# RMS normalisation: other cuts of the first and third tile's loads, and of the first groups

## The chip, the cores and the metric

The kernel runs on one core of a Trainium2 chip. The metric is the device time of one execution in microseconds (us). Three runs of the kernel before gave a median of 161.39 us (161.28 to 161.51). The profile covers one execution of its own; its span of 159.6 us is a little shorter than the time measured for that execution (161.33 us), as it begins and ends with the recorded work.

## The reference

The input x is 16 x 1024 x 512 in float32, gamma has 512 elements. Every row of 512 is divided by its root mean square, and multiplied by gamma:

```python
def reference(x, gamma):
    eps = 1e-5
    rms = np.sqrt(np.mean(x ** 2, axis=-1, keepdims=True) + eps)
    return (x / rms * gamma).astype(np.float32)
```

x is 33.55 MB, and so is the output, so 67.1 MB have to move.

## The kernel before

The 16,384 rows are cut into four tiles (t = 0 to 3), each of 128 partitions with R = 32 rows of 512. In what follows "a row" is one row in each of the 128 partitions, 128 x 512 x 4 bytes = 0.262 MB. Three slots in on-chip memory hold a tile each; tile 3 takes the slot of tile 0 again. Results are written in place, and stored from the slot.

All transfers are issued by SyncE, in the order of the program: one that waits holds back those behind it.

```python
xv = xf.rearrange("(t p r) d -> t p r d", p=P, r=R)
slots = [const.tile([P, R, D], fp32, name=f"slot{i}") for i in range(3)]

def load(t, slot, r0, r1):
    dma = nc.sync.dma_start(out=slots[slot][:, r0:r1], in_=xv[t][:, r0:r1])
    ...
gamma_row = const.tile([1, D], fp32)
pieces = (0, 128, 224, 320, 416, D)

load(0, 0, 0, 8)
for c0, c1 in zip(pieces, pieces[1:]):
    nc.sync.dma_start(out=gamma_row[:, c0:c1], in_=gamma.unsqueeze(0)[:, c0:c1])
load(0, 0, 8, 16)
load(0, 0, 16, 32)
load(1, 1, 0, 16)
load(1, 1, 16, 32)
```

Gamma, one row, is spread to all partitions by a matmul with a column of ones (`gamma_psum`), and copied once to on-chip memory (`gamma_b`) for GpSimd.

The work goes in groups (tile, first row, rows, pieces of the squares, rows for GpSimd):

```python
groups = [
    (0, 0, 7, (7,), 3),
    (0, 7, 9, (9,), 5),
    (0, 16, 16, (7, 9), 7),
    (1, 0, 16, (7, 9), 7),
    (1, 16, 16, (7, 5, 4), 7),
    ...            # (2, 0), (2, 16), (3, 0), (3, 16): 16 rows each, (7, 5, 4)
]
```

ScalarE squares a piece and DVE sums each row of it. The squares need a place: PSUM holds at most 7 rows, a tile of its own 5, and a piece of 9 is parked in the last rows of slot 2, which tile 2 is not yet in.

```python
def square_sums(ss, t, g, r, m, k):
    if m == 9:
        sq = slots[2][:, 23:32, :]
    else:
        home, name, most = ((psum, "sq_psum", 7), (const, "sq_sbuf", 5))[k % 2]
        sq = home.tile([P, most, D], fp32, name=name)
    rows = slots[slot_of[t]][:, g + r : g + r + m, :]
    nc.scalar.activation(out=sq[:, :m], in_=rows, func=AF.Square)
    nc.vector.tensor_reduce(out=ss[:, r : r + m, 0], in_=sq[:, :m], axis=mybir.AxisListType.X, op=OP.add)
```

The group's inverse root is taken by ScalarE (square root) and DVE (reciprocal). GpSimd multiplies the last `share` rows of the group by it and by gamma; for the others ScalarE does the first product, row by row, and DVE the second, with `gamma_psum`, in one instruction. Each engine runs in the order of the program, and the squares of the next group stand ahead of the scaling of this one:

```python
for k, group in enumerate(groups):
    ...
    scale_by_pool(rstd, t, g, n, share)       # GpSimd
    for piece in todo[:2]:
        square_sums(*piece)                   # next group: ScalarE, DVE
    scale(rstd, t, g, 0, half)                # ScalarE
    for piece in todo[2:]:
        square_sums(*piece)
    scale(rstd, t, g, half, mine)             # ScalarE
    times_gamma(t, g, 0, mine)                # DVE
    transfers(t, g)                           # SyncE
    for nxt in ahead:
        rstd = inverse_rms(ss, nxt[2])        # ScalarE, DVE
```

The stores and the later loads:

```python
def transfers(t, g):
    if (t, g) == (0, 0):
        store(0, 0, 0, 1)
        load(2, 2, 0, 16)
        store(0, 0, 1, 2)
        load(2, 2, 16, 23)
    elif (t, g) == (0, 16):
        store(0, 0, 2, 3)
        load(2, 2, 23, 32)
        store(0, 0, 3, 16)
        store(0, 0, 16, 32)
        load(3, 0, 0, 16)
        load(3, 0, 16, 32)
    elif (t, g) == (1, 16):
        store(1, 1, 0, 32)
    elif (t, g) == (2, 16):
        store(2, 2, 0, 32)
    elif (t, g) == (3, 0):
        store(3, 0, 0, 16)
    elif (t, g) == (3, 16):
        store(3, 0, 16, 32)
```

Here the load of tile 2's rows 23 to 32 has to wait until DVE has summed the last piece of 9 squares (group (1, 0)) out of these rows, and the first load of tile 3 until the store of the same rows of tile 0 has landed.

Of the kernel before, what the change touches and what calls it, by code (L numbers as in the profile page):

```python
# [9 lines left out]
def kernel(  # L10
# [6 lines left out]
    nc = tc.nc  # L17
# [8 lines left out]
    N, D = xf.shape  # L26
# [13 lines left out]
    slots = [const.tile([P, R, D], fp32, name=f"slot{i}") for i in range(3)]  # L40
# [3 lines left out]
    def load(t, slot, r0, r1):  # L44
        dma = nc.sync.dma_start(out=slots[slot][:, r0:r1], in_=xv[t][:, r0:r1])
        before_scale.append((slot, r0, r1, dma))

    def store(t, slot, r0, r1):
        dma = nc.sync.dma_start(out=ov[t][:, r0:r1], in_=slots[slot][:, r0:r1])
        before_scale.append((slot, r0, r1, dma))  # L50

    gamma_row = const.tile([1, D], fp32)
    pieces = (0, 128, 224, 320, 416, D)

    load(0, 0, 0, 8)
    for c0, c1 in zip(pieces, pieces[1:]):
        nc.sync.dma_start(out=gamma_row[:, c0:c1], in_=gamma.unsqueeze(0)[:, c0:c1])
    load(0, 0, 8, 16)
    load(0, 0, 16, 32)
    load(1, 1, 0, 16)  # L60
    load(1, 1, 16, 32)

# [11 lines left out]


    groups = [
        (0, 0, 7, (7,), 3),
        (0, 7, 9, (9,), 5),
        (0, 16, 16, (7, 9), 7),
        (1, 0, 16, (7, 9), 7),  # L80
        (1, 16, 16, (7, 5, 4), 7),
        (2, 0, 16, (7, 5, 4), 7),
# [4 lines left out]
    slot_of = [0, 1, 2, 0]  # L87

    def square_sums(ss, t, g, r, m, k):
        if m == 9:  # L90
            sq = slots[2][:, 23:32, :]
        else:
            home, name, most = ((psum, "sq_psum", 7), (const, "sq_sbuf", 5))[k % 2]
            sq = home.tile([P, most, D], fp32, name=name)
        rows = slots[slot_of[t]][:, g + r : g + r + m, :]
        nc.scalar.activation(out=sq[:, :m], in_=rows, func=AF.Square)  # L96
        nc.vector.tensor_reduce(  # L97
            out=ss[:, r : r + m, 0], in_=sq[:, :m], axis=mybir.AxisListType.X, op=OP.add
        )
# [29 lines left out]
    def transfers(t, g):  # L129
        if (t, g) == (0, 0):  # L130
            store(0, 0, 0, 1)
            load(2, 2, 0, 16)
            store(0, 0, 1, 2)
            load(2, 2, 16, 23)
        elif (t, g) == (0, 16):
            store(0, 0, 2, 3)
            load(2, 2, 23, 32)
            store(0, 0, 3, 16)
            store(0, 0, 16, 32)
            load(3, 0, 0, 16)  # L140
            load(3, 0, 16, 32)
        elif (t, g) == (1, 16):
# [7 lines that stand above are left out]
# [12 lines left out]
    for piece in todo:  # L162
        square_sums(*piece)
    rstd = inverse_rms(ss, groups[0][2])
    nc.scalar.copy(out=gamma_b[:, 0], in_=gamma_psum[:, 0])  # L165
    for k, group in enumerate(groups):
        t, g, n, pieces, share = group
        mine = n - share
        half = (mine + 1) // 2
        ahead = groups[k + 1 :][:1]  # L170
        ss, todo = pieces_of(ahead[0]) if ahead else (None, [])
        scale_by_pool(rstd, t, g, n, share)
        for piece in todo[:2]:
            square_sums(*piece)
        scale(rstd, t, g, 0, half)
        for piece in todo[2:]:
            square_sums(*piece)
        scale(rstd, t, g, half, mine)
        times_gamma(t, g, 0, mine)
        transfers(t, g)  # L180
        for nxt in ahead:
            rstd = inverse_rms(ss, nxt[2])
# [30 lines left out]
```

## Time and profile before

| what | value |
|---|---|
| time, median of 3 | 161.39 us |
| profile span | 159.6 us |
| DVE busy | 112.0 us, 70% |
| ScalarE (ACT) busy | 107.8 us, 68% |
| GpSimd (POOL) busy | 106.4 us, 67% |
| TensorE busy | 2.0 us, 1% |
| bytes read and written | 33.56 MB and 33.55 MB |
| mean over the span | 421 GB/s |
| 16 DMA engines' share, SyncE's queue | 98.2% |

An engine's line in the profile has its busy time, its share of the span and its instructions. In the timeline each line has start, duration, engine, line of the kernel, operation, output<-input and shapes; in square brackets stands the idle time before it and what ended it. SPq is SyncE's sequencer: its DMA lines show when a transfer was issued, not when its bytes moved. The DMA view lists issues with the KB of each and the time from issue to landing, that is, until its semaphore is complete. The slices cut the span into 40 equal parts of 4 us; the DMA digit is the busy share in tenths, and GB/s what was moved.

### The profile page before, as it was taken

The page shows a single profiled execution, that of the slowest core. Times are in us where ns is not written, and L with a number is a line of the kernel's source. Part 1 is how long each engine was busy: PE and PEld are TensorE (multiplying, and loading weights), DVE is VectorE, ACT ScalarE, POOL GpSimd, SP SyncE. Part 2 cuts the span into 40 slices and gives each one's busy share as a digit, 9 for nine tenths or more (in the row PEclk, how much of TensorE's full clock was granted, in tenths as well). Part 3 has the DMA queues.
Part 4 walks back from the last instruction along what each step waited for, and adds up shares of the span by engine and source line. Part 5 has one row for each costly group of instructions (what it writes and reads, how often), then busy time and mean ns, then how long its engine had stood idle before and what let it go on. Part 6 is the DMA issues. An engine that isn't in the chain of part 4 may idle for free.

```text
span 159.6 us, 275 instructions
## 1 busy us (share of the span) xinstructions
PE 2.0 (1%) x2; PEld 0.5 (0%) x2; DVE 112.0 (70%) x39; ACT 107.8 (68%) x108; POOL 106.4 (67%) x24
## 2 busy tenths in 40 slices
PE   0050000000000000000000000000000000000000
PEld 0010000000000000000000000000000000000000
DVE  0028097998898999999999999999999009700000
ACT  3072957967999998999899899989960990000000
POOL 1000942994999599999999999999999990000000
DMA  5999999999999999999999999996996997999995
GB/s 199 428 427 501 419 394 435 485 394 394 460 394 394 429 454 407 427 452 452 468 394 394 509 411 394 526 526 263 526 509 279 526 476 312 394 468 452 394 435 222
DMA packets 2747, 67.12 MB, mean 421 GB/s; under 512 B 313, under 2 KB 314, under 8 KB 698
## 3 DMA queue, kind: packets, MB, share of 16 engines
q1 hardware_dynamic: 2746, 67.11, 98.2%
q14 instruction: 1, 0.01, 0.0%
HBM read 33.56 MB, written 33.55 MB: 421 GB/s over the span
## 4 chain that ended last, share of the span: by engine, by line
DVE 59%; ACT 22%; DMA 4%; ACTq 0%; issue 0%
DVE ss L97 36%; DVE slot L122 23%; ACT slot L118 8%; ACT slot L96 7%; ACT sq_psum L96 6%; DMA slot<-in_x_dram 4%; DVE ss L103 1%; ACT ss L102 1%; ACTq L208 0%; ACT gamma_b L165 0%
## 5 line engine op out<-in xcount | busy, mean ns | idle before, releaser
L109 POOL TENSOR_TENSOR slot<-slot,ss 128x3584 f32<-128x3584 f32 (+2 forms) x9 | 46.9, 5214 | 23.7 <-DVE ss L103 23.7
L110 POOL TENSOR_TENSOR slot<-slot,gamma_b 128x3584 f32<-128x3584 f32 (+2 forms) x9 | 59.3, 6585 | 0.7
L97 DVE TENSOR_REDUCE ss<-sq_psum 128x7 f32<-128x3584 f32 (+1 forms) x13 | 42.2, 3246 | 13.2 <-ACT sq_psum L96 13.2
L118 ACT ACTIVATE slot<-slot,ss 128x512 f32<-128x512 f32 x75 | 47.2, 706 | 4.7 <-DVE ss L103 4.7
L122 DVE TENSOR_TENSOR slot<-slot,gamma_psum 128x4608 f32<-128x4608 f32 (+2 forms) x9 | 41.3, 4590 | 8.7 <-ACT slot L118 8.7
L96 ACT ACTIVATE sq_psum<-slot 128x3584 f32<-128x3584 f32 (+1 forms) x13 | 34.6, 2658 | 6.0 <-DMA slot<-in_x_dram 5.2
L97 DVE TENSOR_REDUCE ss<-slot 128x9 f32<-128x4608 f32 x3 | 14.9, 4953 | 4.4 <-ACT slot L96 4.2
L97 DVE TENSOR_REDUCE ss<-sq_sbuf 128x5 f32<-128x2560 f32 x5 | 14.0, 2802 | 0.0
L96 ACT ACTIVATE slot<-slot 128x4608 f32<-128x4608 f32 x3 | 12.1, 4032 | 0.0
L96 ACT ACTIVATE sq_sbuf<-slot 128x2560 f32<-128x2560 f32 x5 | 11.6, 2320 | 0.0
L102 ACT ACTIVATE ss<-ss,eps_t 128x16 f32<-128x16 f32 (+2 forms) x9 | 2.7, 304 | 11.9 <-DVE ss L97 11.9
L103 DVE RECIPROCAL ss<-ss 128x16 f32<-128x16 f32 (+2 forms) x9 | 2.1, 235 | 0.4 <-ACT ss L102 0.4
L66 PE MATMUL gamma_psum<-gamma_row,ones_col 1*128 1x512 f32 x2 | 2.0, 1121 | 8.7 <-DMA gamma_row<-in_gamma_dram 8.7
L72 ACT ACT_TABLE_LOAD x1 | 1.3, 1283 | 1.1 <-PEq L197 1.1
L165 ACT COPY gamma_b<-gamma_psum 128x512 f32<-128x512 f32 x1 | 0.6, 564 | 0.0
L66 PEld LDWEIGHTS gamma_psum<-gamma_row,ones_col 1*128 1x128 f32 x2 | 0.5, 304 | 8.7 <-issue 8.7
L64 POOL MEMSET ones_col<- 1x128 f32 x1 | 0.2, 194 | 0.3 <-POOLq L197 0.3
L197 POOL MEMSET const-float32-0.0<- 128x1 f32 x1 | 0.1, 98 | 0.2 <-issue 0.2
L72 ACT ACTIVATE table<-eps_t 128x1 f32<-128x1 f32 x1 | 0.2, 203 | 0.0
L197 POOL MEMSET const-bfloat16-1.0<- 128x1 bf16 x1 | 0.1, 101 | 0.0
L197 POOL MEMSET const-uint8-127<- 128x1 uint8 x1 | 0.1, 101 | 0.0
L197 POOL MEMSET const-float32-1.0<- 128x1 f32 x1 | 0.1, 98 | 0.0
(1 smaller groups left out, 0.1 us busy)
## 6 DMA issues: line engine op xcount, KB each, us to landing
slot<-in_x_dram SPq DMA_DIRECT2D x6, 4096.0 KB, 21.7
out_dram<-slot SPq DMA_DIRECT2D x3, 4096.0 KB, 21.9
slot<-in_x_dram SPq DMA_DIRECT2D x2, 2048.0 KB, 8.5
out_dram<-slot SPq DMA_DIRECT2D x1, 3328.0 KB, 21.7
slot<-in_x_dram SPq DMA_DIRECT2D x1, 2304.0 KB, 14.2
slot<-in_x_dram SPq DMA_DIRECT2D x1, 1792.0 KB
out_dram<-slot SPq DMA_DIRECT2D x3, 256.0 KB, 29.4
gamma_row<-in_gamma_dram SPq DMA_DIRECT2D x4, 0.4 KB
```

The costliest lines, as they stand in the source:

```text
L66: nc.tensor.matmul(gamma_psum[:, 0], ones_col, gamma_row, start=True, stop=True)
L72: nc.scalar.activation(out=table, in_=eps_t, func=AF.Sqrt)
L96: nc.scalar.activation(out=sq[:, :m], in_=rows, func=AF.Square)
L97: nc.vector.tensor_reduce(out=ss[:, r : r + m, 0], in_=sq[:, :m], axis=mybir.AxisListType.X, op=OP.add)
L102: nc.scalar.activation(out=ss[:, :n, 0], in_=ss[:, :n, 0], func=AF.Sqrt, bias=eps_t, scale=1.0 / D)
L103: nc.vector.reciprocal(out=ss[:, :n, 0], in_=ss[:, :n, 0])
L109: nc.gpsimd.tensor_tensor(out=part, in0=part, in1=by_row, op=OP.mult)
L110: last = nc.gpsimd.tensor_tensor(out=part, in0=part, in1=gamma_b.to_broadcast([P, share, D]), op=OP.mult)
L118: nc.scalar.activation(out=x[:, g + r, :], in_=x[:, g + r, :], func=AF.Copy, scale=rstd[:, r])
L122: scaled = nc.vector.tensor_tensor(out=part, in0=part, in1=gamma_psum.to_broadcast([P, r1 - r0, D]), op=OP.mult)
L165: nc.scalar.copy(out=gamma_b[:, 0], in_=gamma_psum[:, 0])
L197: nc = _bacc.Bacc("TRN2", target_bir_lowering=False, num_devices=1)
```

## The change

The change makes fewer and larger transfers in the beginning. Tile 0 comes in 12 and 20 rows in place of 8, 8 and 16. Its groups have 12, 10 and 10 rows in place of 7, 9 and 16, and two of them use pieces of 10 squares, which are parked in slot 2's last rows, 22 to 32, as the pieces of 9 are in 23 to 32. Gamma is one transfer in place of five. Of the three early single-row stores one is left. Tile 2 comes in 20 and 12 rows in place of 16, 7 and 9, the 20 after the first group and the 12 after the last group of tile 0. The stores of tile 0's other rows are cut at row 22 in place of row 16.

```diff
     gamma_row = const.tile([1, D], fp32)
-    pieces = (0, 128, 224, 320, 416, D)
-
-    load(0, 0, 0, 8)
-    for c0, c1 in zip(pieces, pieces[1:]):
-        nc.sync.dma_start(out=gamma_row[:, c0:c1], in_=gamma.unsqueeze(0)[:, c0:c1])
-    load(0, 0, 8, 16)
-    load(0, 0, 16, 32)
+
+    load(0, 0, 0, 12)
+    nc.sync.dma_start(out=gamma_row, in_=gamma.unsqueeze(0))
+    load(0, 0, 12, 32)
     load(1, 1, 0, 16)
     load(1, 1, 16, 32)
 ...
     groups = [
-        (0, 0, 7, (7,), 3),
-        (0, 7, 9, (9,), 5),
-        (0, 16, 16, (7, 9), 7),
+        (0, 0, 12, (7, 5), 5),
+        (0, 12, 10, (10,), 5),
+        (0, 22, 10, (10,), 5),
         (1, 0, 16, (7, 9), 7),
 ...
     def square_sums(ss, t, g, r, m, k):
-        if m == 9:
-            sq = slots[2][:, 23:32, :]
+        if m > 7:
+            sq = slots[2][:, 32 - m : 32, :]
 ...
         if (t, g) == (0, 0):
             store(0, 0, 0, 1)
-            load(2, 2, 0, 16)
-            store(0, 0, 1, 2)
-            load(2, 2, 16, 23)
-        elif (t, g) == (0, 16):
-            store(0, 0, 2, 3)
-            load(2, 2, 23, 32)
-            store(0, 0, 3, 16)
-            store(0, 0, 16, 32)
+            load(2, 2, 0, 20)
+        elif (t, g) == (0, 22):
+            load(2, 2, 20, 32)
+            store(0, 0, 1, 22)
+            store(0, 0, 22, 32)
             load(3, 0, 0, 16)
             load(3, 0, 16, 32)
```

## The prediction

> **What bounds the kernel now.** I read the page's slices and totals first, then the DMA issues one by one, then the timeline of the first 56 us. A row below means one row per partition: 128 x 512 floats, 0.262 MB, and the kernel moves 128 rows in and 128 rows out.
>
> ```profile
> DMA  5999999999999999999999999996996997999995
> GB/s 199 428 427 501 419 394 435 485 394 394 460 394 394 429 454 407 427 452 452 468 394 394 509 411 394 526 526 263 526 509 279 526 476 312 394 468 452 394 435 222
> ...
> HBM read 33.56 MB, written 33.55 MB: 421 GB/s over the span
> ```
>
> The DMA digits are 9 nearly everywhere. A single slice is not to be believed (526 beside 263 GB/s: whole packets are counted in one slice or the next), but the mean is. DVE, ScalarE and GpSimd are at 67 to 70%. The page's chain that ended last runs through DVE and ScalarE, because it follows semaphores back from the last store; it does not show that the store's bytes queued behind others. So I look at when each transfer lands. From the DMA views of short windows (size, then us from issue to landing), in order of issue:
>
> ```profile
> slot<-in_x_dram SPq DMA_DIRECT2D x1, 2048.0 KB, 7.1
> ...
> slot<-in_x_dram SPq DMA_DIRECT2D x1, 2048.0 KB, 9.8
> ...
> slot<-in_x_dram SPq DMA_DIRECT2D x1, 4096.0 KB, 19.2
> ...
> out_dram<-slot SPq DMA_DIRECT2D x1, 256.0 KB, 29.4
> ...
> slot<-in_x_dram SPq DMA_DIRECT2D x1, 2304.0 KB, 14.2
> ...
> out_dram<-slot SPq DMA_DIRECT2D x1, 4096.0 KB, 20.0
> ```
>
> Their issues stand in the timeline of SyncE at 0.74, 2.90, 3.29, 28.80, 49.40 and 138.76 us. Issue plus time to landing gives the landings, and summing the rows in program order gives how many rows had then gone through the queue: 8 rows at 7.84, 16 at 12.7, 32 at 22.5, 90 at 58.2, 99 at 63.6, and all 256 at 158.8. One straight line through first and last fits all: **landing of row n = 2.98 + 0.609 n us** (7.85, 12.7, 22.5, 57.8, 63.3, 158.9). A queue that had once run empty would have left a step. The kernel is bound by one queue that is never empty, at 0.262 MB / 0.609 us = 430 GB/s, and compute is hidden.
>
> The first load gives the cost of a cold start: 7.1 us for 8 rows, of which 8 x 0.609 = 4.87 is streaming and 2.23 is fixed. A transfer issued at t with n rows ahead of it therefore keeps to the line if t + 2.23 is no later than 2.98 + 0.609 n, that is, **issued by D(n) = 0.75 + 0.609 n**. The transfer to watch is the last piece of tile 2, which cannot be issued before DVE has summed the squares that were parked in its rows:
>
> ```profile
> 24.61 2.28 DVE L122 TENSOR_TENSOR slot<-slot,gamma_psum 128x2048 f32<-128x2048 f32 x1
> ...
> 24.94 3.14 ACT L96 ACTIVATE sq_psum<-slot 128x3584 f32<-128x3584 f32 x1
> ...
> 26.92 0.35 SPq L49 DMA_DIRECT2D out_dram<-slot  x1
> ...
> 40.36 4.03 ACT L96 ACTIVATE slot<-slot 128x4608 f32<-128x4608 f32 x1
> ...
> 44.42 4.95 DVE L97 TENSOR_REDUCE ss<-slot 128x9 f32<-128x4608 f32 x1
> ...
> 49.40 0.33 SPq L45 DMA_DIRECT2D slot<-in_x_dram  x1
> ```
>
> The reduce ends at 44.42 + 4.95 = 49.37 and the load is issued at 49.40. Ninety rows are ahead of it (64 of loads, then 1, 16, 1, 7 and 1), so D(90) = 55.6: 6.2 us to spare. That spare time is what hides the wait today.
>
> **What the Trainium skill says.** "DMA: Bandwidth & Descriptors", section Where 436 GB/s comes from, gives a ceiling of 435.2 GB/s for a core's DMA; the 430 GB/s of the line is within about 1% of it, so the only thing the change can win in the stream is about 67.1 MB / 435.2 = 154.2 against 256 x 0.609 = 155.9, 1.7 us. The same page, Anatomy of one DMA, says that any wait for a semaphore takes place on the issuing sequencer before dispatch; the trace agrees (the load is issued 0.03 us after the reduce), and it means that everything behind a waiting load in program order waits too. "SBUF — State Buffer", The DMA setup-cost knee, has about 2 us that don't scale with bytes; measured here, 2.23.
>
> **The change part by part.** Durations: ScalarE squares 3.14 us for 7 rows and 4.03 for 9, so 0.445 a row and 4.47 for 10; 2.32 for 5. DVE sums 3.83 to 3.89 for 7, 4.95 for 9, so 0.55 a row and 5.5 for 10; 2.80 for 5. DVE's product with gamma 2.28 for 4 rows, 4.94 for 9: 0.53 a row, 3.88 for 7, 2.81 for 5. ScalarE scales a row in 0.63.
>
> *Gamma in one piece* takes four issues of about 0.33 us off SyncE, 1.3 us in which the queue had 8 rows (4.9 us) to work on. The landings at 16 and 32 rows lie on the line, so the five pieces cost nothing visible. Worth: 0.
>
> *Loads in 12 and 20 rows.* The same bytes; but work waits for the whole of each. Twelve rows land at 2.98 + 7.31 = 10.3 (8 landed at 7.84, +2.4). The next 20 land together at row 32: 22.5, where rows 8 to 16 used to be there at 12.7. Step by step, in program order:
> - First group: squares of 7 rows 10.3 to 13.5, of 5 rows to 15.8; DVE sums 13.5 to 17.3 and to 20.1; root and reciprocal to 20.7 (15.5 before).
> - Second group: ScalarE would be free at 20.9 but its rows land at 22.5. Squares of 10 rows 22.5 to 27.0, sum 27.0 to 32.5, then the product with gamma of the first group's 7 rows 32.4 to 36.3 (it ended at 26.9 before).
> - The store of row 0 is issued at 36.3 and the 20-row load of tile 2 at 36.7, not at 26.9 and 27.3. With 64 rows ahead, D(64) = 39.7: 3.4 us to spare. No gap here.
> - Third group: ScalarE's root at 32.5, squares of 10 rows 32.7 to 37.2, sum 37.2 to 42.7, root, then tile 1's first 7 squares from 42.9 to 46.1 and its 9 squares, which are parked in tile 2's last rows, from 46.0 to 50.05. DVE sums the 7 until 50.0 and the 9 from 50.1 to **55.0** (49.37 before, +5.7).
>
> *Third tile in 20 and 12 rows, one early store.* The 12-row load waits for that sum and is issued at 55.06. Ahead of it lie 64 + 1 + 20 = 85 rows, 5 fewer than before, so D(85) = 52.5. **It is 2.55 us late**, and the queue is empty for that long: the 21-row and 10-row stores stand behind it on SyncE and can't fill the hole, although most of their rows are done.
>
> *Small stores.* Two fewer transfers of 2 KB per partition. The landings after the three early stores lie 0.3 to 0.4 us above the line (58.2 for 57.8; 63.6 for 63.3), so two of them may save 0.2.
>
> *After the hole.* The shift of compute: DVE's product for the third group is 5 rows, not 9, and ends at 58.2 instead of 54.9 (+3.3); ScalarE is 5.7 later when it begins tile 1's second half (55.7 for 50.0). Both engines are nearly full, so later groups run 3.3 to 5.7 us later. Does that open a second hole? The queue itself is 2.55 later. The first load of tile 3 goes when the 21-row store has landed: 118 rows, 2.98 + 71.9 + 2.55 = 77.4, against D(128) + 2.55 = 81.3. The store of tile 2 was issued at 111.19, so by 116.9, against D(192) + 2.55 = 120.2. The last store by 138.76 + 5.7 = 144.5 against D(240) + 2.55 = 149.5. All keep 3 us or more: no second hole, and none of the spare time gives the first one back.
>
> Sum: 161.39 + 2.55 - 0.2 = **163.7 us**, 1.4% slower.
>
> **Rivals.** (1) *The hole is hidden and the time stays at 161.4.* For it: the margin is a difference of two numbers near 54, and 2 us of error in either closes it; a somewhat slower stream in the first 50 us would do it (the landings run 0.4 late there). Against it: eight steps of the chain have measured durations, and only the 10-row forms are extrapolated, by one row. (2) *A second hole or a longer one*: if ScalarE's shift passes fully to the stores of tiles 2 and 3, or if the 36.7 us load misses its 3.4 us, each 1 us more adds 1 us: 165 or more. (3) *Faster*: fewer, larger transfers push the stream towards the ceiling. At most 1.7 us, if there were no hole at all: 159.7. The before's line leaves so little that over 2% (158.2 us) is out of reach. (4) *Compute becomes the bound*: it would need the last store's issue after 149.5; estimated at 144.5, so no.
>
> **Range and chances.** The chain of steps I trust to 0.7 us, the landing line to 0.4, a restart in mid-stream (both directions busy) to perhaps 0.5. That makes 162.2 to 165.0. Slower by over 2% begins at 164.6: one chance in seven. Faster by over 2%: one in a hundred.
>
> **What would show it.** In the changed kernel's trace: first squares at 10.3, second group's at 22.5 and waiting for a load; row 0's store at 36.3; the sum of the 9 squares ending at 55.0 and the 12-row load issued right after it; that load landing 9.5 us after issue (2.23 + 12 x 0.609), cold, instead of queued; landings on the old line before it and 2.4 us above it up to the last. The prediction is wrong if landings stay on one line (rival 1), or if a second step shows at tile 2's or tile 3's stores (rival 2).

## The result, and the profile after

The changed kernel takes **165.53 us** (165.51 to 165.58), 4.1 us more than before; the ratio is 1.0256 with an interval of 1.0239 to 1.0274. That is slower by over 2%, and above the predicted range of 162.2 to 165.0.

The page of the changed kernel, busy share and rate of the DMA engines in slices of 4.1 us:

```profile
DMA  5999999999999399999999999999989969899994
GB/s 194 468 429 480 440 416 392 440 456 384 384 480 480 96 408 264 504 431 410 400 440 440 400 456 424 448 448 512 416 352 512 480 288 512 384 400 464 416 432 208
```

The 14th slice (53.2 to 57.3 us) has a 3 and 96 GB/s where the digit was 9 before: here the queue ran empty. A slice counts a packet where it begins (a full share of 1.78 stands beside an empty slice further below), so its width is not to be taken from here.

The timeline of the changed kernel: start, duration, engine, operation.

```profile
10.59 3.16 ACT L93 ACTIVATE sq_psum<-slot 128x3584 f32<-128x3584 f32 x1 [7.95 <-DMA slot<-in_x_dram]
...
22.70 4.47 ACT L93 ACTIVATE slot<-slot 128x5120 f32<-128x5120 f32 x1 [1.50 <-DMA slot<-in_x_dram]
...
50.29 4.95 DVE L94 TENSOR_REDUCE ss<-slot 128x9 f32<-128x4608 f32 x1
...
36.52 0.35 SPq L49 DMA_DIRECT2D out_dram<-slot  x1
...
55.27 0.33 SPq L45 DMA_DIRECT2D slot<-in_x_dram  x1
```

All of compute's steps stand within 0.3 us of where they were predicted: 10.6 for 10.3, 22.7 for 22.5 with ScalarE idle for 1.50 us on the 20-row load, 36.5 for 36.3, and the sum of the nine squares ends at 55.24 for 55.0. The late load is issued at 55.27.

What differs is the landings. From the DMA view of the changed kernel, the 20-row load issued at 36.91, the late load (55.27), the 21-row store behind it (55.70), and the last store (143.38):

```profile
slot<-in_x_dram SPq DMA_DIRECT2D x1, 5120.0 KB, 18.0
...
slot<-in_x_dram SPq DMA_DIRECT2D x1, 3072.0 KB, 11.0
...
out_dram<-slot SPq DMA_DIRECT2D x1, 5376.0 KB, 23.4
...
out_dram<-slot SPq DMA_DIRECT2D x1, 4096.0 KB, 19.5
```

Row 85 lands at 54.9 (the old line says 54.7), row 97 at 66.3 (62.1), row 118 at 79.1 (74.8), row 256 at 162.9 (158.9). So **one step, between rows 85 and 97**: 11.4 us from landing to landing, where 12 rows take 7.3. It is 4.1 us, as much as the time that was lost; after it the landings run beside the old line, 4.0 to 4.6 us above it.

The first load of this kernel, issued at 0.74, also brings 12 rows and also starts with nothing ahead of it:

```profile
slot<-in_x_dram SPq DMA_DIRECT2D x1, 3072.0 KB, 9.8
```

So the late load, with 11.0 us, is 1.2 us slower than a cold start of its own size. The 9.5 us expected for it came from the first load of the kernel before, and that load's fixed part of 2.23 us is at the low end: in the sixteen traces of this case the first load's time less 0.609 us a row is 2.2 to 2.6 us, here 9.8 - 7.3 = 2.5.

### The profile page after: what moved, and what is told of

Read it like the earlier page. It is cut to its first block, busy times and chain, and to the rows that moved or that the text cites. A ratio compares the mean times of both kernels' runs of the same rounds, so it can differ in the third digit from the quotient of the medians.

```text
span 163.8 us, 260 instructions
## 1 busy us (share of the span) xinstructions
PE 2.0 (1%) x2; PEld 0.5 (0%) x2; DVE 112.2 (69%) x39; ACT 107.9 (66%) x108; POOL 106.4 (65%) x24
## 4 chain that ended last, share of the span: by engine, by line
DVE 51%; ACT 23%; DMA 13%; SPq 0%; ACTq 0%; issue 0%
DVE ss L94 31%; DVE slot L119 19%; DMA slot<-in_x_dram 13%; ACT slot L115 8%; ACT slot L93 8%; ACT sq_psum L93 5%; ACT sq_sbuf L93 1%; ACT ss L99 1%; DVE ss L100 1%; ACTq L202 0%; SPq L45 0%; SPq L55 0%
## 5 line engine op out<-in xcount | busy, mean ns | idle before, releaser
L94 DVE TENSOR_REDUCE ss<-sq_psum 128x7 f32<-128x3584 f32 (+1 forms) x12 | 38.4, 3200 | 15.3 <-ACT sq_psum L93 15.3
L119 DVE TENSOR_TENSOR slot<-slot,gamma_psum 128x4608 f32<-128x4608 f32 (+3 forms) x9 | 41.3, 4590 | 8.3 <-ACT slot L115 8.3
L93 ACT ACTIVATE sq_psum<-slot 128x3584 f32<-128x3584 f32 (+1 forms) x12 | 31.4, 2616 | 8.6 <-DMA slot<-in_x_dram 7.9
L94 DVE TENSOR_REDUCE ss<-slot 128x10 f32<-128x5120 f32 (+1 forms) x3 | 15.9, 5308 | 7.1 <-ACT slot L93 7.0
L94 DVE TENSOR_REDUCE ss<-sq_sbuf 128x5 f32<-128x2560 f32 x6 | 16.8, 2804 | 0.0
L93 ACT ACTIVATE slot<-slot 128x5120 f32<-128x5120 f32 (+1 forms) x3 | 12.9, 4317 | 1.5 <-DMA slot<-in_x_dram 1.5
L93 ACT ACTIVATE sq_sbuf<-slot 128x2560 f32<-128x2560 f32 x6 | 13.9, 2320 | 0.0
```

Of the source, the lines that this page charges most:

```text
L119: scaled = nc.vector.tensor_tensor(out=part, in0=part, in1=gamma_psum.to_broadcast([P, r1 - r0, D]), op=OP.mult)
```

## The experiments

To compare runs I use that step: the time from the landing of the transfer ahead to the landing of the late load, less 0.609 us a row. "Late by" is the issue time plus the cold start's fixed 2.23 us, less the landing of the transfer ahead; negative if the load came in time. With a fixed part of 2.5 us all these figures would be 0.3 us larger.

**Fill the empty stretch.** The 21-row store, ready long before, goes ahead of the late load:

```diff
-            load(2, 2, 20, 32)
             store(0, 0, 1, 22)
+            load(2, 2, 20, 32)
```

> Theory (the loss is one empty stretch of the queue behind the late 12-row load, with the slow restart that follows it): the 21-row store, ready at about 47 us, goes ahead of that load, so 106 rows are ahead of it and it may be issued up to 65.3 us; it is issued near 55.3, nothing runs empty, and all of the 4.1 us comes back: 161.4 us, within 0.4. Rival (about half of the loss lies in other parts of the change: one gamma transfer, fewer early stores, larger pieces): 163 us or more.

162.11 us, ratio 1.0034 (1.0017 to 1.0051). The store is issued at 46.77, the load still at 55.19, and the DMA view of this kernel shows it queued behind other work:

```profile
out_dram<-slot SPq DMA_DIRECT2D x1, 5376.0 KB, 21.6
...
slot<-in_x_dram SPq DMA_DIRECT2D x1, 3072.0 KB, 20.2
```

From the store's landing (68.37) to the load's (75.39) is 7.02 us for 12 rows: no step. 3.6 of the 4.1 us come back with nothing changed but the order of two transfers, and the rival, that half of the loss lies in the pieces, falls. Half a microsecond stays, a little more than the 0.4 that the theory allowed. It is not lost at the late load: this kernel's landings lie 0.4 us above the line at row 85, ahead of that load, and 1.1 us above it at row 144.

**More or fewer rows ahead of the late load.** Tile 2 in 22 and 10 rows, or 16 and 16:

```diff
-            load(2, 2, 0, 20)
+            load(2, 2, 0, 22)        # second kernel: 0, 16
 ...
-            load(2, 2, 20, 32)
+            load(2, 2, 22, 32)       # second kernel: 16, 32
```

> The early load of tile 2 takes 22 rows and the late one 10, nothing else changes. Theory (lateness plus a fixed slow restart of 1.4 us): two more rows ahead shorten the empty stretch by 2 x 0.609 = 1.2 us: 164.3 us. Rival (the slow restart grows with the length of the empty stretch): more than 1.2 us comes back, 163.8 us or less. Rival (the loss is elsewhere): no change, 165.5.

164.11 us, ratio 1.0137 (1.0051 to 1.0222). Late by 1.4, step 2.6.

> The early load of tile 2 takes 16 rows and the late one 16. Theory: four rows fewer ahead lengthen the empty stretch by 4 x 0.609 = 2.4 us: 168.0 us, with the slow restart still about 1.4 us of it. Rival (slow restart in proportion): 169.3 us. Rival (the loss is elsewhere): 165.5.

167.93 us, ratio 1.037 (1.0298 to 1.0442). Late by 5.0, step 6.5. Over these three kernels (20, 22 and 16 rows) the step is the lateness plus 1.2 to 1.5 us, whatever the lateness is: a fixed extra, which the prediction didn't have.

**An earlier late load.** Tile 0 in three loads, so that the second group needn't wait for row 32:

```diff
-    load(0, 0, 12, 32)
+    load(0, 0, 12, 22)
+    load(0, 0, 22, 32)
```

> Tile 0 comes in 12, 10 and 10 rows, so that the second group's rows land near 16.5 us and not 22.7. Theory: ScalarE begins the second group at 20.9, 1.8 us earlier, every step up to the late load moves with it, the load is issued at 53.5 and not 55.3, and 1.8 us comes back: 163.7 us. Rival (the second group isn't what sets the late load): 165.5 us.

164.94 us, ratio 1.0184 (1.0113 to 1.0255). The chain of steps moved as expected: the second group's squares begin at 21.01, the late load is issued at 53.58, 1.7 us earlier. But only 0.6 us came back (0.8 if each kernel is compared with the runs of the kernel before beside it). The load took 12.2 us from issue to landing, not 11.0: late by 0.8, step 3.4. The fixed extra was no longer fixed.

**What the extra belongs to.** In the changed kernel the windows of 1 us show where the late load loses it. Columns: busy time of PE, PEld, DVE, ACT and POOL, then TensorE's clock, the DMA engines' share and GB/s.

```profile
61.00:62.00 1.00, 0.00 (x0) 0.00 (x0) 1.00 (x1) 1.00 (x2) 1.00 (x1) 1.00 0.92 393
62.00:63.00 1.00, 0.00 (x0) 0.00 (x0) 1.00 (x2) 1.00 (x3) 1.00 (x1) 1.00 1.78 393
63.00:64.00 1.00, 0.00 (x0) 0.00 (x0) 1.00 (x1) 1.00 (x3) 1.00 (x1) 1.00 0.00 0
64.00:65.00 1.00, 0.00 (x0) 0.00 (x0) 1.00 (x1) 1.00 (x1) 0.92 (x2) 1.00 1.46 393
```

Each filled window holds the same bytes: one packet of 24 KB, the 12 rows of one partition, on each of the 16 DMA engines (16 x 24.6 KB = 393 KB). Call this a round. The rounds take 0.92 us of the engines' time at first, and 1.78 and 1.46 in the last two rounds before the store: 1.4 us more. Four kernels change what stands behind the late load, or the load itself:

```diff
-            store(0, 0, 1, 22)
+            store(0, 0, 1, 12)        # 11 and 10 rows
+            store(0, 0, 12, 22)
```

> The store of 21 rows that stands behind the late 12-row load is cut into 11 and 10. In the changed kernel this load took 11.0 us from issue to landing, 1.46 more than the cold start's 2.23 + 12 x 0.609 = 9.54. Theory S1 (the 1.46 us come from the large store right behind, in proportion to its pieces): about half goes, landing after 10.3 us and 164.8 us in all. S2 (a fixed cost of a restart that turns from a load to a store) and S3 (the store's being issued 0.4 us after the load, into an empty queue): no change, 11.0 us and 165.5.

165.67 us; the load lands after 10.9 us. Size of the store (S1): no.

```diff
             load(2, 2, 20, 32)
+            store(0, 0, 22, 24)       # not ready before 58 us
             store(0, 0, 1, 22)
-            store(0, 0, 22, 32)
+            store(0, 0, 24, 32)
```

> Between the late load and the 21-row store stands a store of rows 22 and 23, which isn't ready before 58.0 us; so the stores are issued 2.8 us after the load and not 0.4. S3: the load lands after 9.5 us and the time falls by about 1.4, to 164.1. S1: the 2-row store takes the place behind the load; most of the 1.46 us goes as well. S2: 11.0 us and 165.5.

165.47 us; the load lands after 10.9 us, with the stores issued 2.7 us behind it. S3, the store's being issued at once: no.

```diff
-            store(0, 0, 1, 22)
+            store(0, 0, 1, 2)
+            store(0, 0, 2, 22)
```

> The 21-row store is cut into 1 and 20 rows; the single row is issued 0.4 us after the late load. S1 (size of the store right behind): the load lands after 9.6 us, the time falls to about 164.2. S2 and S3: 11.0 us, 165.5.

165.61 us; 10.9 us again. S1 falls a second time.

```diff
-            load(2, 2, 20, 32)
+            load(2, 2, 20, 26)
+            load(2, 2, 26, 32)
```

> The late 12-row load is cut into two of 6 rows, issued 0.4 us apart, the store behind them. If the slow part belongs to the turn from loads to stores (S1, S2), the first 6 rows land cold after 2.23 + 3.65 = 5.9 us and the second piece carries the whole 1.46: the two together as before, 165.5 us. If it belongs to a load that is alone in an empty queue, the first piece carries it: 7.3 us.

165.66 us. The first six rows land after 6.5 us (0.6 over the cold start), all twelve 11.8 us after the first issue, 2.2 over the cold start's 9.54 and not 1.46 (this profiled execution took 166.05 us, 0.4 over the median). Most of the extra is in the second piece. Next, a single-row store between the two pieces:

```diff
             load(2, 2, 20, 26)
+            store(0, 0, 1, 2)
             load(2, 2, 26, 32)
-            store(0, 0, 1, 22)
+            store(0, 0, 2, 22)
```

> Behind the empty stretch the queue gets 6 rows of load, a single-row store, 6 rows of load, and then the 20-row store: two turns from load to store. If the first turn after a restart pays (S2), the first 6 rows land after about 5.9 + 1.5 = 7.4 us, and the second turn pays little. If only the turn to a long run of stores pays, the first 6 rows land after 5.9 to 6.5 us and the second 6 carry it. The time stays near 165.6 in both; if both turns pay, 167.

165.63 us, and the first six rows land after 6.9 us, between what the two theories expected. The landing alone doesn't decide; the windows of 2 us do better. First the kernel with two pieces and no store between them, then the one with the store:

```profile
58.00:60.00 2.00, 0.00 (x0) 0.00 (x0) 1.60 (x1) 2.00 (x2) 2.00 (x1) 1.00 1.00 399
60.00:62.00 2.00, 0.00 (x0) 0.00 (x0) 2.00 (x1) 2.00 (x4) 2.00 (x1) 1.00 1.16 418
62.00:64.00 2.00, 0.00 (x0) 0.00 (x0) 2.00 (x2) 2.00 (x4) 2.00 (x1) 1.00 0.90 252
```

```profile
58.00:60.00 2.00, 0.00 (x0) 0.00 (x0) 1.47 (x2) 2.00 (x2) 1.90 (x1) 1.00 0.98 301
60.00:62.00 2.00, 0.00 (x0) 0.00 (x0) 2.00 (x1) 2.00 (x4) 2.00 (x1) 1.00 1.01 418
62.00:64.00 2.00, 0.00 (x0) 0.00 (x0) 2.00 (x2) 2.00 (x4) 2.00 (x1) 1.00 1.08 444
```

The slow stretch (252 GB/s at 62 to 64) is gone from its place and stands at 58 to 60 (301), ahead of the single-row store; the turn to the 20-row store is then at full rate. The later landings agree: at the single-row store (row 92, 62.8 us) they are 3.8 us above the line, and at the 20-row store (row 118, 78.7 us) 3.9. So the slow rounds go with the first turn from load to store after the restart, even where that store is one row.

**Restart with a store.** Both stores go ahead of the late load, the one that isn't ready first:

```diff
-            load(2, 2, 20, 32)
-            store(0, 0, 1, 22)
             store(0, 0, 22, 32)
+            store(0, 0, 1, 22)
+            load(2, 2, 20, 32)
```

> The two stores go ahead of the late load, the 10-row one first. It isn't ready before 58.0 us, with 85 rows ahead of it (D = 52.5), so the queue is empty for about 5.4 us and restarts with stores; a load follows them. If the slow 1.4 us belongs to the turn from load to store after a restart, there is none here: the 10-row store lands after 2.2 + 6.1 = 8.3 us and the time is about 161.5 + 0.5 + 5.4 = 167.4. If any restart in mid-stream costs it, the store lands after 9.7 us and the time is 168.8.

167.63 us, ratio 1.0376 (1.0361 to 1.0391), and the first store lands 7.5 us after its issue, 10 rows of which are 6.1. The first store, and the second, issued at 58.41:

```profile
out_dram<-slot SPq DMA_DIRECT2D x1, 2560.0 KB, 7.5
...
out_dram<-slot SPq DMA_DIRECT2D x1, 5376.0 KB, 20.8
```

The queue was empty for as long as with tile 2 in 16 and 16 rows or longer (late by 5.4), and the restart itself has no extra: the step at the first store is 4.5 us, less than the lateness, since this store has 1.4 us of fixed time and not 2.23. But two later turns lose time. From the first store's landing (65.5) to the second's (79.3) 13.7 us pass for 21 rows that need 12.8; behind these stores stands a load. And from tile 3's first load (96.3) to its second (106.9) 10.6 us pass for 16 rows that need 9.7; behind these loads stands a store, in a full queue. In the changed kernel the same two stretches take 12.8 and 9.7 us. So it is luck that the time meets the 167.4 us of the theory: the first store landed 0.8 us sooner than the 8.3 that it assumed, and the two turns then lost 0.9 us each.

**The small parts, alone, in the kernel before.**

```diff
-    pieces = (0, 128, 224, 320, 416, D)
+    pieces = (0, D)
```

> The kernel before with gamma in one transfer, nothing else. Theory: the five pieces cost nothing that can be seen, 161.5 us, the same as before within 0.3. Rival: they are part of what the change lost or won, over 0.5 us either way.

161.89 beside 161.63, ratio 1.0032 (1.001 to 1.0054).

```diff
-            store(0, 0, 1, 2)
-            store(0, 0, 2, 3)
-            store(0, 0, 3, 16)
+            store(0, 0, 1, 16)
```

> The kernel before with one early single-row store; rows 1 and 2 go with the later store of tile 0, 1 to 16. Ninety rows ahead of the late load become 88, it may be issued up to 54.3 and is issued at 49.4: no empty stretch. By the prediction two small stores fewer save 0.2: 161.3 us. Rival: the half microsecond that stays when the empty stretch is filled comes from the missing small stores: 162.0 us.

161.79 beside 161.63, ratio 1.0013 (1.0003 to 1.0023). By the medians each costs a little, 0.26 and 0.16 us; by the intervals it is 0.1 to 0.5% for gamma and 0.03 to 0.2% for the stores. Together the medians make 0.42 of the 0.53 that stayed when the empty stretch was filled. That they add up so is arithmetic and not a run.

**Does it take an empty queue?** Tile 0 in three loads and tile 2 in 22 and 10 rows, and the same with three rows in the early store (89 rows ahead, not 87); the late load and the late store begin where these end:

```diff
-            store(0, 0, 0, 1)
-            load(2, 2, 0, 20)
+            store(0, 0, 0, 1)         # second kernel: 0, 3
+            load(2, 2, 0, 22)
```

> Tile 0 in 12, 10 and 10 rows (the late load is issued at 53.6) and tile 2 in 22 and 10 (87 rows ahead, D = 53.7, with the 0.2 us that landings were late 53.9). The load comes about 0.3 us before the queue would run empty. If the slow turn needs an empty queue, everything comes back but half a microsecond: 162.1 us. If it only needs a load that is issued with little left ahead of it, the load lands 1.2 us or more above the line and the time is 163.3 or more.

164.37 us, ratio 1.0191 (1.0152 to 1.023).

> The same, with an early store of three rows and not one: 89 rows ahead, so the late load has about 1.5 us to spare. Theory (empty queue): 162.1 us, as with 0.3 to spare. If a short queue is enough for the slow turn, this run lies below the one with 0.3 us to spare: 162 against 163.

162.25 us, ratio 1.004 (1.0025 to 1.0055). The DMA view of both, first with 87 rows ahead, then with 89: the transfer ahead (issued at 35.38 and 35.34) and the late load (53.75 and 53.71).

```profile
slot<-in_x_dram SPq DMA_DIRECT2D x1, 5632.0 KB, 20.9
...
slot<-in_x_dram SPq DMA_DIRECT2D x1, 2560.0 KB, 11.5
```

```profile
slot<-in_x_dram SPq DMA_DIRECT2D x1, 5632.0 KB, 22.6
...
slot<-in_x_dram SPq DMA_DIRECT2D x1, 2560.0 KB, 10.4
```

From landing to landing 8.9 us against 6.1 (from the trace; the view rounds to 0.1), for ten rows that need 6.09. In the first kernel the load came 0.3 us in time and lost 2.8; in the second 2.0 us in time (by its own landings, the transfer ahead being a little late too), and lost nothing. So the deadline D(n), from the fixed part of the first load, was too generous; with 2.5 us in place of 2.23 the first of the two loads comes just at the deadline. All the kernels with a late load in one piece and a store behind it, in order of how late the load was:

| kernel | issued, us | late by, us | step in the landings, us | time over before, us |
|---|---|---|---|---|
| three loads, 22 and 10, three-row store | 53.71 | -2.0 | 0.0 | 0.6 |
| three loads, 22 and 10 | 53.75 | -0.3 | 2.8 | 2.8 |
| three loads, 20 and 12 | 53.58 | 0.8 | 3.4 | 3.4 |
| two loads, 22 and 10 | 55.32 | 1.4 | 2.6 | 2.5 |
| the change, store in 11 and 10 rows | 55.28 | 2.2 | 3.6 | 4.2 |
| the change, two-row store between | 55.13 | 2.2 | 3.6 | 4.0 |
| the change, store in 1 and 20 rows | 55.12 | 2.5 | 3.9 | 4.1 |
| the change | 55.27 | 2.6 | 4.1 | 4.1 |
| two loads, 16 and 16 | 55.29 | 5.0 | 6.5 | 6.4 |

In five rows the last two columns agree within 0.1 us. In the other four the time is longer by 0.6, 0.6, 0.4 and 0.2 us (in the table's order), and these traces show 0.55, 0.4, 0.4 and 0.2 us lost earlier, between the landings of rows 48 and 64, ahead of the first store. With some 2 us to spare nothing is lost; about the deadline 2.8 are lost at once; beyond it the loss is the lateness plus 1.2 to 2.6.

## Why the prediction was wrong, step by step

**What bounds the kernel, and where it would break:** right. The landings lay on one line before; the only step in the changed kernel is at the 12-row load of tile 2, behind the sum of the nine parked squares.

**The chain of compute up to that load:** right to 0.3 us in every step (55.27 for 55.06), the extrapolated 10-row forms included: 4.47 and 5.49 us measured for 4.47 and 5.5.

**"It is 2.55 us late, and the queue is empty for that long":** the lateness was right, 2.6 by the changed kernel's own landings. The step that failed is the next one, taking the lateness for the loss. The term of 2.55 us in the sum measured 4.1, so 1.5 us were missing, and "a restart in mid-stream to perhaps 0.5" was the width given to it. D(n) came from the first load of the kernel, which has 2.23 us of fixed time. That load has more loads behind it, 64 rows in all, and its number was used for a load of 12 rows with stores behind. The late load took 11.0 us, not 9.5. Of this difference 0.3 us is in the cold start itself (the first load of the changed kernel has 2.5 us of fixed time and not 2.23), and 1.2 us stand against that load of the same 12 rows; the slow rounds are its last two, ahead of the stores. With the lateness and that extra the sum is 161.4 + 2.6 + 1.5 = 165.5.

**No second hole:** right. The first load of tile 3 was issued at 79.08, the store of tile 2 at 115.50 and the last at 143.38, all in time; the landings after row 97 show no second step.

**Two small stores fewer, -0.2, and gamma, 0:** the first is wrong in sign and the second was not quite 0, both at a small size. Taken alone they cost 0.16 and 0.26 us.

**The rivals:** the hidden hole (1) is out. "A longer hole" (2) is the direction in which it went, but not by its causes: neither tile 3's stores nor the 36.7 us load had a part. Nothing became faster (3); the 1.7 us given for it, an estimate, were not put to a test. Compute (4) never became the bound.

**What stays open:** why a load near the end of an emptying queue is slow, and slow ahead of the first store. Shown is where the extra stands: ahead of the first store behind the late load, whatever that store's size or the moment of its issue, and earlier when the store comes earlier. A restart with stores has none at the restart, though two later turns of that kernel lost 0.9 us each, one of them in a full queue. By the deadline used here the extra begins 0.3 us before the queue runs dry; with a fixed part of 2.5 us it begins at that moment. At the kernel's start a load also begins cold, and in the changed kernel the turn to the first store, at row 65, costs next to nothing (9.8 us from row 48 to row 64, which need 9.7); in the kernel with the three-row store the same rows took 10.3. One reading is that loads normally run ahead of what has landed, which covers a slow turn, and that a late load has no such lead; no run shows that lead. A late load with only loads behind it was not run, so that the store is needed for the extra rests on the one pair of kernels with two pieces. Nor is it shown why three loads of tile 0 made the extra larger (2.6) than two (1.2 to 1.5).

## What to carry to other kernels

When one queue sets the time, write down the landings with the bytes ahead of each, and look for the transfer with the least to spare: its engine chain decides, not the mean load of any engine. A transfer that waits holds up the ready ones behind it, so put ready transfers ahead of the one that waits; here two exchanged lines gave back 3.6 of 4.1 us. Leave a late load a margin, here 2 us beyond the moment at which the queue would run dry by a cold start's time, because missing it costs more than the lateness. With 0.3 us of margin 2.8 us were lost, and nothing between the two was tried.

## What the runs showed of the hardware that was not expected

A load issued 0.3 us before its computed deadline lost 2.8 us, almost as much as one 0.8 us after it (3.4), and, in the kernels with tile 0 in two loads, more than one 1.4 us after it (2.6). After an empty stretch the same load packets took 1.78 and 1.46 us in the two rounds ahead of a store, where 0.92 is usual. A restart with stores landed 10 rows in 7.5 us, 1.4 over their streaming time and less than a load's 2.2 to 2.6, but two later turns between stores and loads then lost 0.9 us each.
